# Hybrid decoder trunk, first stage: dt from raw x in fp32 on four column groups, and C's first tile beside B's

## The chip, the cores and the metric

The kernel runs on one core of a Trainium2 chip. The metric is device time in microseconds (us) of one execution of the whole program; a median over several runs is given. A profile is one further execution, recorded by the hardware profiler, with its own time. The engines are TensorE (PE, matrix products; PEld is its weight load), VectorE (DVE), ScalarE (ACT), GpSimd (POOL) and SyncE (SP), which here only starts transfers.

## The reference, cut to what matters

One layer of a decoder trunk: 528 tokens (16 learned meta tokens, then 512) of width 1024.

```python
u = rmsnorm(h, mix_norm_w[i])              # h * rsqrt(mean(h*h) + eps) * w
proj = u @ w_in[i]                         # 1024 x 9248
z = proj[..., OFF_Z:OFF_XBC]
xbc = proj[..., OFF_XBC:OFF_DT]            # x (2048), B (8 x 128), C (8 x 128)
dt_raw = proj[..., OFF_DT:OFF_GATE]        # 32 heads
gates = jax.nn.sigmoid(proj[..., OFF_GATE:] + b_gate[i])
...
xbc = jax.nn.silu(causal_depthwise_conv(xbc, conv_w, conv_b))
dt = jax.nn.softplus(dt_raw + dt_bias)
a_dt = dt * -jnp.exp(a_log)                # its cumulative sum per chunk of 128 is acs
y = ssd_chunked(xs, dt, a, b_mat, c_mat) + xs * d_skip[:, None]
...
h = h + (gate_pool * y_pool + gate_ssd * y_ssd) @ w_o[i]
v = rmsnorm(h, mlp_norm_w[i])
h = h + jax.nn.relu(v @ w_ff1[i]) ** 2 @ w_ff2[i]
out = rmsnorm(h, final_norm_w)[:, N_META:]
```

All is fp32.

## The kernel before, in words

**How products are made.** Activations lie transposed, channels on the partitions, in 8 tiles of 128 channels x 528 tokens. Most products are made from two halves: a value is cast to a shorter type (fp32r, "hi"), the rest is kept too ("lo"), and hi x hi, hi x lo and lo x hi are added in PSUM. So one product of 128 channels by 128 columns by a run of tokens is three matmuls. Weights come in blocks of 128 x 1024 (512 KB) in the order of use: `block_part` (L70) starts the transfer on SP's queue, ACT casts to `whi` (L73) and DVE subtracts to `wlo` (L74). Three raw blocks and four pairs of halves can be under way.

**The first stage.** Before the norm is known, projections run on x times the norm's weight (`xh`, `xl`, made from `xt` in `x_split`, L194 and L195) and are multiplied by the per-token scale `rsb` afterwards. Nine products of ones (L187) run while the first loads come. Then a loop over the 8 channel tiles k (L208 to L227): load `xt[k]`, split it, multiply it into `pdt` (dt) and `pB` (the first tile of B), and square it for the norm's sum `q` (on ACT and DVE). dt has only 32 columns of weights; they are repeated four times to fill 128 (`spread`, `once`, L184 to L208), so that all four chunks of 128 tokens find their dt on the partitions on which they are used. `dt_runs` are two runs of 272 and 256 tokens.

After the loop C's tile (`px0_24`), two tiles of x (`px0_0`, `px0_1`), z (`pz0`) and `GATES_FIRST` gates (`pgp`) follow on PE as group 0. Into them are woven, in the order in which a scheduler sees them ready: the sum of squares (`pn`, L244), the scale's broadcast (`pb`, L262, copied to `rsb` by ACT in L264), then DVE's chain for dt: `dv` (dt times the scale, L278 and L279), a softplus by a polynomial (L285 to L294, `ddt`), the cumulative sums (`dacs`, L299), and PE's transposes of both (`pt_dt`, L305). `norm_u` (L323 to L325) makes the normed `uh` and `ul` that all later projections read.

**After it.** For the groups g = 0 to 7 the state-space part of group g is woven with the projections of group g+1 (`px`, `pz`), and with one more gate where `GATE_AT` names one. L470 in there multiplies two heads of 64 channels into the two halves of one PSUM tile (`py`), in fp32. Pooling, the output product and the MLP follow.

**What sets the order.** Each engine works through its own list in order; the lists are made by a scheduler from the program's order and its own estimates, so a change in one place moves instructions around it. PSUM has two tiles of two banks (`psum2`: px, pz, pgp, pB) and four of one bank (`psum1`: pdt, pn, pb, pt_dt). SP starts transfers in order, POOL only a few.

Of the kernel before, what the change touches and what calls it, by code (L numbers as in the profile page):

```python
# [9 lines left out]
F32 = mybir.dt.float32  # L10
F32R = mybir.dt.float32r
AF = mybir.ActivationFunctionType
ALU = mybir.AluOpType

P = 128
D = 1024
SEQ = 512
NM = 16
# [18 lines left out]
V_N = 234  # L37


GATES_FIRST = 3  # L40
GATE_AT = {1: 3, 2: 4, 3: 5, 5: 6}
POOL_ORDER = (3, 2, 1, 0)
MERGE = (0, 4, 1, 5, 2, 6, 3, 7)

# [5 lines left out]
def kernel(ctx: ExitStack, tc, xT, x, w, vec, fnw, out):  # L50
# [12 lines left out]
    def block_tiles():  # L63
        b = nblk[0]
        nblk[0] += 1
        return (b, wp.tile([P, 1024], F32, tag="raw", name=f"raw{b}", bufs=3),
                wp.tile([P, 1024], F32R, tag="whi", name=f"whi{b}"),
                wp.tile([P, 1024], F32R, tag="wlo", name=f"wlo{b}"))

    def block_part(t, c):  # L70
        b, raw, hi, lo = t
        nc.sync.dma_start(raw[:, c], w[b, :, c])
        act.copy(hi[:, c], raw[:, c])  # L73
        dve.tensor_tensor(lo[:, c], raw[:, c], hi[:, c].bitcast(F32), op=ALU.subtract)  # L74

# [57 lines left out]
    def psum2(name):  # L133
        return psa.tile([P, 1024], F32, tag="mm", name=name)

    def psum1(name):
        return psb.tile([P, 512], F32, tag="s", name=name)
# [14 lines left out]
    def wide(ps, skip=0):  # L152

        h = (L - skip) // 2
        runs = [(ps[:, 512 - h : 512], slice(skip, skip + h)),
                (ps[:, 512 : 512 + h], slice(skip + h, L))]
        return runs, ps[:, 512 - h : 512 + h]
# [14 lines left out]
    H = HEADS  # L172


    pdt = [psum1(f"pdt{i}") for i in range(2)]
    dt_runs = [(pdt[0][:, : NM + 256], slice(0, NM + 256)), (pdt[1][:, :256], slice(NM + 256, L))]
    pB = psum2("px0_16")
    runsB, viewB = wide(pB)

    wdt, wB = block_tiles(), block_tiles()  # L180
    b, raw, hi, lo = wdt
    nc.sync.dma_start(raw[:, :256], w[b, :, :256])
    spread = lambda t: t.rearrange("p (k c h) -> p k c h", c=4, h=HEADS)
    once = raw[:, :256].rearrange("p (k h) -> p k h", h=HEADS).unsqueeze(2).to_broadcast([P, NK, 4, HEADS])  # L184

    for n in range(WARM):
        pe.matmul(pdt[1].rearrange("p (a b) -> p a b", a=4), ones_r,  # L187
# [2 lines left out]
    def x_load(k):  # L190
        nc.sync.dma_start(xt[k], xT[:, k, :])

    def x_split(k):
        act.activation(xh[k], xt[k], AF.Copy, scale=col(V_MIX, k))  # L194
        dve.scalar_tensor_tensor(xl[k], xt[k], col(V_MIX, k), xh[k].bitcast(F32),  # L195
                                 op0=ALU.mult, op1=ALU.subtract)

    x_load(0)
    act.copy(spread(hi)[:, :2], once[:, :2])
    dve.tensor_tensor(spread(lo)[:, :2], once[:, :2], spread(hi)[:, :2].bitcast(F32), op=ALU.subtract)  # L200
    x_split(0)
    block_part(wB, slice(0, 256))
    x_load(1)
    proj_step(dt_runs, 0, wdt[2:], X)
    proj_step(runsB, 0, wB[2:], X)
    x_split(1)
    act.copy(spread(hi)[:, 2:], once[:, 2:])
    dve.tensor_tensor(spread(lo)[:, 2:], once[:, 2:], spread(hi)[:, 2:].bitcast(F32), op=ALU.subtract)  # L208
    x_load(2)
    block_part(wB, slice(256, 1024))  # L210
    proj_step(dt_runs, 1, wdt[2:], X)
    proj_step(runsB, 1, wB[2:], X)
    def square(k):
        if k == 0:
            act.activation(q, xt[k], AF.Square)
# [5 lines left out]
    for k in range(2, NK):  # L221
        if k > 2:
            x_load(k)
        x_split(k)
        proj_step(dt_runs, k, wdt[2:], X)
        proj_step(runsB, k, wB[2:], X)
        square(k - 2)  # L227
    for k in (NK - 2, NK - 1):
        square(k)

# [43 lines left out]
    v, e, s, s2, pl, dt, acs = (dtile(n) for n in ("dv", "de", "ds", "ds2", "dpl", "ddt", "dacs"))  # L274
    for c in range(4):
        r = slice(c * H, (c + 1) * H)
        src = pdt[0][r, NM + c * P : NM + (c + 1) * P] if c < 2 else pdt[1][r, (c - 2) * P : (c - 1) * P]
        dve.tensor_tensor(v[r, :P], src, rsb[r, NM + c * P : NM + (c + 1) * P], op=ALU.mult)  # L278
    dve.tensor_tensor(v[:, P:], pdt[0][:, :NM], rsb[:, :NM], op=ALU.mult)  # L279
    act.activation(e, v, AF.Abs, bias=col(V_DTB, 0))  # L280
    act.activation(e, e, AF.Exp, scale=-1.0)
    ea = dp.tile([P, 1], F32, name="ea")
# [68 lines left out]
    def group_proj(g, cur, gate=None):  # L351

        first = g == 0
        xc, bt, ct, zt = cur
        for dst, t, skip in ((bt, 16 + g, 0), (ct, 24 + g, NM - 4), (xc[:, 0, :], 2 * g, 0),
                             (xc[:, 1, :], 2 * g + 1, 0)):
            if first and dst is bt:
                view = viewB
            else:
                runs, view = wide(psum2(f"px{g}_{t}"), skip)  # L360
                proj(runs, block(), X if first else U)
            conv(dst, first_raw(t, view, skip) if first else view, t)
            yield
        if gate is not None:
            gate_pool(gate)
            yield
        ps = psum2(f"pz{g}")
        for i in range(2):
            proj(narrow(ps[:, i * SEQ : (i + 1) * SEQ]), block(), X if first else U)
        zf = zt.rearrange("p i t -> p (i t)")  # L370
        if first:
            dve.tensor_tensor(zt, ps.rearrange("p (i t) -> p i t", i=2),
                              rsb[:, NM:].unsqueeze(1).to_broadcast([P, 2, SEQ]), op=ALU.mult)
            act.activation(zf, zf, AF.Silu)
        else:
            act.activation(zf, ps, AF.Silu)
        yield
# [829 lines left out]
```

## Time and profile before

| | us |
|---|---|
| median of 3 runs | 1025.1 (1024.82 to 1025.12) |
| the profiled execution | 1024.72 |
| its span, first to last instruction | 1023.0 |
| k loop of the first stage, first dt product to first C product | 5.5 to 18.3 |
| gates of the first stage, first product of `pgp` | 50.1 |
| first transposes of group 0 (L413) | 67.3 |
| PE, DVE, ACT busy | 1014.7, 739.4, 553.0 |

The granted clock of TensorE is 0.999 of full over the run. Views of the profile give times from the start of the span. A row of the timeline holds start, duration, engine, line, operation, output and inputs, sizes and count, and in brackets the idle time before it with what ended it. A q behind an engine is its instruction queue (SPq starts transfers). Matmuls overlap, so that the distance between starts, not the duration, is what one costs. A view by stretch gives, for each window, its length, then busy time and instructions of PE, PEld, DVE, ACT and POOL, the clock, and DMA. Waits are listed as total, count and longest.

### The profile page before, as it was taken

What the parts mean: (1) busy time and instruction counts of PE and PEld (TensorE: products, weight loads), DVE (VectorE), ACT (ScalarE), POOL (GpSimd) and SP (SyncE); (2) the same over time, 40 slices, a digit from 0 to 9 for tenths busy, and PEclk for the clock granted to TensorE, in tenths of its full rate; (3) what the DMA queues carried; (4) which work ended last, traced back from release to release, by engine and by line L of the source; (5) the groups of instructions that cost most, each with busy time, mean ns of one, the idle gap of its engine ahead of it and who ended that gap; (6) DMA issues with size and microseconds to landing.
All of it is one profiled execution on the core that took longest, in us unless ns stands there. A gap on an engine that the chain in (4) does not pass through costs nothing.

```text
span 1023.0 us, 14052 instructions
## 1 busy us (share of the span) xinstructions
PE 1014.7 (99%) x5697; PEld 878.0 (86%) x5697; DVE 739.4 (72%) x982; ACT 553.0 (54%) x728; POOL 9.9 (1%) x24
## 2 busy tenths in 40 slices
PE   9999999999999999999999999999999999999997
PEld 9889989998879898988899888888888888888886
DVE  7978788687746586978755457976686686776866
ACT  7775968586627339573244343475545355454444
POOL 0100000000000000000000001000000000000000
PEclk9999999999999999999999999999999999999999
DMA  6243051414332331414532333224323323334112
GB/s 238 72 159 104 21 165 41 146 46 140 103 102 85 103 104 42 145 42 140 189 102 85 103 104 119 87 90 157 103 83 106 121 82 112 96 102 124 42 42 83
DMA packets 29281, 105.62 MB, mean 103 GB/s; under 512 B 3297, under 2 KB 4257, under 8 KB 28193
## 3 DMA queue, kind: packets, MB, share of 16 engines
q1 hardware_dynamic: 26496, 92.75, 28.7%
q0 software_dynamic: 2000, 11.08, 2.9%
q8 instruction: 45, 0.74, 0.3%
q10 hardware_dynamic: 720, 0.91, 0.2%
q14 instruction: 20, 0.16, 0.0%
HBM read 102.55 MB, written 2.16 MB: 102 GB/s over the span
## 4 chain that ended last, share of the span: by engine, by line
PE 97%; DVE 2%; ACT 0%; issue 0%; ACTq 0%
PE px L143 6%; PE px L144 6%; PE pf L92 6%; PE px L146 6%; PE pf L91 6%; PE pf L90 6%; PE alpha L956 3%; PE alpha L957 3%; PE alpha L958 3%; PE pz L143 3%; PE pz L146 3%; PE pz L144 3%; PE py L470 2%; PE pso L90 2%; PE pp L144 2%; PE pp L146 2%
## 5 line engine op out<-in xcount | busy, mean ns | idle before, releaser
L73 ACT CAST whi<-raw 128x1024 fp32r<-128x1024 f32 (+1 forms) x131 | 135.7, 1043 | 231.5 <-PE pf L91 58.8
L74 DVE TENSOR_TENSOR wlo<-raw,whi 128x1024 fp32r<-128x1024 f32 (+1 forms) x131 | 158.4, 1212 | 125.1 <-ACT whi L73 117.8
L143 PE MATMUL px<-uh,whi 128*128 128x264 f32 (+1 forms) x448 | 121.2, 290 | 0.7 <-DVE ct L334 0.7
L144 PE MATMUL px<-ul,whi 128*128 128x264 f32 (+1 forms) x448 | 119.0, 286 | 0.0
L90 PE MATMUL pf<-vh,whi 128*128 128x512 f32 x256 | 99.8, 390 | 0.0
L92 PE MATMUL pf<-vh,wlo 128*128 128x512 f32 x256 | 99.7, 389 | 0.0
L91 PE MATMUL pf<-vl,whi 128*128 128x512 f32 x256 | 99.6, 389 | 0.0
L146 PE MATMUL px<-uh,wlo 128*128 128x264 f32 (+1 forms) x448 | 90.8, 284 | 0.0
L143 PEld LDWEIGHTS px<-uh,whi 128*128 128x128 f32 x448 | 84.6, 189 | 2.8 <-issue 2.6
L144 PEld LDWEIGHTS px<-ul,whi 128*128 128x128 f32 x448 | 84.9, 189 | 0.3
L146 PEld LDWEIGHTS px<-uh,wlo 128*128 128x128 f32 x448 | 69.4, 188 | 0.3 <-issue 0.3
L718 DVE TENSOR_TENSOR slo<-b,shi 128x1024 fp32r<-128x1024 f32 x35 | 42.6, 1217 | 31.7 <-ACT shi L717 31.7
L717 ACT CAST shi<-b 128x1024 fp32r<-128x1024 f32 x35 | 36.8, 1051 | 51.9 <-PE pf L91 36.5
L91 PEld LDWEIGHTS pf<-vl,whi 128*128 128x128 f32 x256 | 48.1, 188 | 10.0
L90 PEld LDWEIGHTS pf<-vh,whi 128*128 128x128 f32 x256 | 48.1, 188 | 9.9
L92 PEld LDWEIGHTS pf<-vh,wlo 128*128 128x128 f32 x256 | 48.1, 188 | 9.9
L956 PE MATMUL alpha<-shi,hh 128*128 128x512 f32 x140 | 54.6, 390 | 0.0
L957 PE MATMUL alpha<-slo,hh 128*128 128x512 f32 x140 | 54.5, 389 | 0.0
L958 PE MATMUL alpha<-shi,hl 128*128 128x512 f32 x140 | 54.5, 389 | 0.0
L783 DVE TENSOR_TENSOR ht<-ht,alpha 128x1024 f32<-128x1024 f32 x35 | 42.5, 1214 | 6.1 <-PE alpha L958 6.1
L143 PE MATMUL pz<-uh,whi 128*128 128x512 f32 x112 | 44.0, 393 | 0.0
L144 PE MATMUL pz<-ul,whi 128*128 128x512 f32 x112 | 43.9, 392 | 0.0
(412 smaller groups left out, 2451.4 us busy)
## 6 DMA issues: line engine op xcount, KB each, us to landing
raw<-in_w SPq DMA_DIRECT2D x129, 512.0 KB, 3.6
b<-in_w SPq DMA_DIRECT2D x28, 512.0 KB, 3.6
abc<-acs_d POOLq DMA_DIRECT2D x8, 1024.0 KB, 7.2
wob<-in_w SPq DMA_DIRECT2D x8, 512.0 KB, 4.6
xt<-in_xT SPq DMA_DIRECT2D x8, 264.0 KB, 5.3
ht<-in_x POOLq DMA_DIRECT2D x4, 512.0 KB, 6.0
w<-in_w SPq DMA_DIRECT2D x4, 512.0 KB, 3.5
out_dram<-out SPq DMA_DIRECT2D x4, 320.0 KB, 2.3
```

The lines of the kernel that those rows point to most:

```text
L73: act.copy(hi[:, c], raw[:, c])
L74: dve.tensor_tensor(lo[:, c], raw[:, c], hi[:, c].bitcast(F32), op=ALU.subtract)
L90: pe.matmul(ps, ah, bh, start=first, stop=False)
L91: pe.matmul(ps, ah, bl, start=False, stop=False)
L92: pe.matmul(ps, al, bh, start=False, stop=last)
L143: pe.matmul(o, wh, rhs[0][k][:, c], start=k == 0, stop=False)
L144: pe.matmul(o, wh, rhs[1][k][:, c], start=False, stop=False)
L146: pe.matmul(o, wl, rhs[0][k][:, c], start=False, stop=k == NK - 1)
L718: dve.tensor_tensor(lo, src, hi.bitcast(F32), op=ALU.subtract)
L956: pe.matmul(ps[t], a[0], wh[:, cs], start=f, stop=False, skip_group_check=True)
L957: pe.matmul(ps[t], a[0], wl[:, cs], start=False, stop=False, skip_group_check=True)
L958: pe.matmul(ps[t], a[1], wh[:, cs], start=False, stop=l, skip_group_check=True)
```

## The change

dt's weights are loaded unsplit and once (128 x 8 x 32, `wdt`), DVE multiplies them by the norm's weight, and dt is made from raw `xt` in plain fp32: in `dt_step`, after k = 3 and k = 7, the four channel tiles of a half of the loop write four different groups of 32 PSUM partitions, for two runs of 264 tokens (`HF`). Each group of partitions then holds the sum over two channel tiles. ACT copies the result to SBUF (`dtp`), and 8 small fp32 products with `e32` (four stacked 32 x 32 identities, made on DVE) add the four groups and put each chunk where it is used (`pdv`), from which `dv` is read.

In the k loop C's first tile takes dt's place beside B's (`bc_step`), with C's weights loaded and split in pieces of 256, 256 and 512 columns as B's now are, between the loads of x. dt's weights are asked for behind the second pieces. The tables of gates change, so that one more gate is computed in the first stage, from x, and none in the stage of group 5.

```diff
--- before.py
+++ after.py
@@ -37,8 +37,8 @@
 V_N = 234
 
 
-GATES_FIRST = 3
-GATE_AT = {1: 3, 2: 4, 3: 5, 5: 6}
+GATES_FIRST = 4
+GATE_AT = {1: 4, 2: 5, 3: 6}
 POOL_ORDER = (3, 2, 1, 0)
 MERGE = (0, 4, 1, 5, 2, 6, 3, 7)
 
@@ -67,9 +67,15 @@
                 wp.tile([P, 1024], F32R, tag="whi", name=f"whi{b}"),
                 wp.tile([P, 1024], F32R, tag="wlo", name=f"wlo{b}"))
 
+    def block_load(t, c):
+        nc.sync.dma_start(t[1][:, c], w[t[0], :, c])
+
     def block_part(t, c):
+        block_load(t, c)
+        block_split(t, c)
+
+    def block_split(t, c):
         b, raw, hi, lo = t
-        nc.sync.dma_start(raw[:, c], w[b, :, c])
         act.copy(hi[:, c], raw[:, c])
         dve.tensor_tensor(lo[:, c], raw[:, c], hi[:, c].bitcast(F32), op=ALU.subtract)
 
@@ -172,16 +178,19 @@
     H = HEADS
 
 
+
+    HF = (slice(0, HALF), slice(HALF, L))
     pdt = [psum1(f"pdt{i}") for i in range(2)]
-    dt_runs = [(pdt[0][:, : NM + 256], slice(0, NM + 256)), (pdt[1][:, :256], slice(NM + 256, L))]
-    pB = psum2("px0_16")
-    runsB, viewB = wide(pB)
-
-    wdt, wB = block_tiles(), block_tiles()
-    b, raw, hi, lo = wdt
-    nc.sync.dma_start(raw[:, :256], w[b, :, :256])
-    spread = lambda t: t.rearrange("p (k c h) -> p k c h", c=4, h=HEADS)
-    once = raw[:, :256].rearrange("p (k h) -> p k h", h=HEADS).unsqueeze(2).to_broadcast([P, NK, 4, HEADS])
+    pB, pC = psum2("px0_16"), psum2("px0_24")
+    (runsB, viewB), (runsC, viewC) = wide(pB), wide(pC, NM - 4)
+    b = nblk[0]
+    nblk[0] += 1
+    wdt = pre.tile([P, NK, H], F32, name="wdt")
+    wB, wC = block_tiles(), block_tiles()
+    e32 = pre.tile([P, H], F32, name="e32")
+    dve.tensor_tensor(e32, ident[:, :H], ident[:, H : 2 * H], op=ALU.add)
+    for c in (2, 3):
+        dve.tensor_tensor(e32, e32, ident[:, c * H : (c + 1) * H], op=ALU.add)
 
     for n in range(WARM):
         pe.matmul(pdt[1].rearrange("p (a b) -> p a b", a=4), ones_r,
@@ -195,21 +204,29 @@
         dve.scalar_tensor_tensor(xl[k], xt[k], col(V_MIX, k), xh[k].bitcast(F32),
                                  op0=ALU.mult, op1=ALU.subtract)
 
+    def dt_step(kb):
+
+        for i, run in enumerate(HF):
+            for c in range(4):
+                k = kb + c
+                pe.matmul(pdt[i][c * H : (c + 1) * H, :HALF], wdt[:, k, :], xt[k][:, run],
+                          start=kb == 0, stop=kb == 4, skip_group_check=True)
+
+    def bc_step(k):
+        proj_step(runsB, k, wB[2:], X)
+        proj_step(runsC, k, wC[2:], X)
+
     x_load(0)
-    act.copy(spread(hi)[:, :2], once[:, :2])
-    dve.tensor_tensor(spread(lo)[:, :2], once[:, :2], spread(hi)[:, :2].bitcast(F32), op=ALU.subtract)
     x_split(0)
-    block_part(wB, slice(0, 256))
+    for t in (wB, wC):
+        block_part(t, slice(0, 256))
     x_load(1)
-    proj_step(dt_runs, 0, wdt[2:], X)
-    proj_step(runsB, 0, wB[2:], X)
+    bc_step(0)
     x_split(1)
-    act.copy(spread(hi)[:, 2:], once[:, 2:])
-    dve.tensor_tensor(spread(lo)[:, 2:], once[:, 2:], spread(hi)[:, 2:].bitcast(F32), op=ALU.subtract)
     x_load(2)
-    block_part(wB, slice(256, 1024))
-    proj_step(dt_runs, 1, wdt[2:], X)
-    proj_step(runsB, 1, wB[2:], X)
+    for t in (wB, wC):
+        block_part(t, slice(256, 512))
+    bc_step(1)
     def square(k):
         if k == 0:
             act.activation(q, xt[k], AF.Square)
@@ -222,9 +239,23 @@
         if k > 2:
             x_load(k)
         x_split(k)
-        proj_step(dt_runs, k, wdt[2:], X)
-        proj_step(runsB, k, wB[2:], X)
+        if k == 2:
+            nc.sync.dma_start(wdt.rearrange("p k h -> p (k h)"), w[b, :, : NK * H])
+            dve.tensor_tensor(wdt, wdt, vs[:, V_MIX : V_MIX + NK].unsqueeze(2).to_broadcast([P, NK, H]), op=ALU.mult)
+        if k == 4:
+            for t in (wB, wC):
+                block_part(t, slice(512, 1024))
+        bc_step(k)
+        if k % 4 == 3:
+            dt_step(k - 3)
         square(k - 2)
+    dts_ = pre.tile([P, L], F32, name="dtp")
+    for i, run in enumerate(HF):
+        act.copy(dts_[:, run], pdt[i][:, :HALF])
+    pdv = psum1("pdv")
+    for o, n, at in ((0, P, lambda c: NM + c * P), (P, NM, lambda c: 0)):
+        for c in range(4):
+            pe.matmul(pdv[c * H : (c + 1) * H, o : o + n], e32, dts_[:, at(c) : at(c) + n], start=True, stop=True)
     for k in (NK - 2, NK - 1):
         square(k)
 
@@ -274,9 +305,8 @@
     v, e, s, s2, pl, dt, acs = (dtile(n) for n in ("dv", "de", "ds", "ds2", "dpl", "ddt", "dacs"))
     for c in range(4):
         r = slice(c * H, (c + 1) * H)
-        src = pdt[0][r, NM + c * P : NM + (c + 1) * P] if c < 2 else pdt[1][r, (c - 2) * P : (c - 1) * P]
-        dve.tensor_tensor(v[r, :P], src, rsb[r, NM + c * P : NM + (c + 1) * P], op=ALU.mult)
-    dve.tensor_tensor(v[:, P:], pdt[0][:, :NM], rsb[:, :NM], op=ALU.mult)
+        dve.tensor_tensor(v[r, :P], pdv[r, :P], rsb[r, NM + c * P : NM + (c + 1) * P], op=ALU.mult)
+    dve.tensor_tensor(v[:, P:], pdv[:, P : P + NM], rsb[:, :NM], op=ALU.mult)
     act.activation(e, v, AF.Abs, bias=col(V_DTB, 0))
     act.activation(e, e, AF.Exp, scale=-1.0)
     ea = dp.tile([P, 1], F32, name="ea")
@@ -354,8 +384,8 @@
         xc, bt, ct, zt = cur
         for dst, t, skip in ((bt, 16 + g, 0), (ct, 24 + g, NM - 4), (xc[:, 0, :], 2 * g, 0),
                              (xc[:, 1, :], 2 * g + 1, 0)):
-            if first and dst is bt:
-                view = viewB
+            if first and (dst is bt or dst is ct):
+                view = viewB if dst is bt else viewC
             else:
                 runs, view = wide(psum2(f"px{g}_{t}"), skip)
                 proj(runs, block(), X if first else U)
```

In the changed program the order on PE is: the k loop with the first dt step behind k = 3 and the second behind k = 7; `px0_0`, into which the 8 small products and `pn` are put after its first 8 matmuls and `pb` after 24 more; `px0_1`; `pz0`, with the transposes of `ddt` after 43 of its 48 matmuls; four gates. On ACT the order behind the last square is the copies of B's and C's PSUM tiles, one weight cast, the two copies of dt. On DVE the steps between `dv` and `ddt` are, beside the chain itself, four raw multiplications by `rsb`, eleven convolution steps, one product of `norm_u` and one weight split; before the change they were four, eight, three and one.

## The prediction

> **What bounds the kernel now.** I read the engine shares first, then the chain that ended last, then who TensorE (PE) waited for.
>
> ```profile
> span 1023.0 us, 14052 instructions
> PE 1014.7 (99%) x5697; PEld 878.0 (86%) x5697; DVE 739.4 (72%) x982; ACT 553.0 (54%) x728; POOL 9.9 (1%) x24
> ...
> PE 97%; DVE 2%; ACT 0%; issue 0%; ACTq 0%
> ```
>
> ```profile
> PE pdt L187 <- DVE ones_r L100: 1.5, 1, 1.5
> PE px L143 <- DVE ct L334: 0.7, 1, 0.7
> PE pt_dt L305 <- DVE ddt L294: 0.2, 1, 0.2
> ```
>
> PE holds 97% of the chain, and all its waits together are 2.4 us. So PE time that is taken away shows in the end one for one, and time that is added too, unless another engine is late. The second and third waits are the only places where DVE is late.
>
> The stage of the change, in the timeline (start, duration, engine, line):
>
> ```profile
> 16.83 0.29 PE L143 MATMUL pdt<-xh,whi 128*128 128x272 f32 x1
> ...
> 17.55 0.28 PE L143 MATMUL px<-xh,whi 128*128 128x264 f32 x1
> ...
> 18.27 0.28 PE L143 MATMUL px<-xh,whi 128*128 128x258 f32 x1
> ...
> 18.99 0.28 PE L143 MATMUL px<-xh,whi 128*128 128x258 f32 x1
> ...
> 20.54 1.09 PE L244 MATMUL pn<-ones_f,q 128*88 128x1 f32 x12
> 21.49 0.36 PE L144 MATMUL px<-xl,whi 128*128 128x258 f32 x1
> ...
> 25.54 0.28 PE L143 MATMUL px<-xh,whi 128*128 128x264 f32 x1
> ...
> 31.41 0.28 PE L143 MATMUL px<-xh,whi 128*128 128x264 f32 x1
> ```
>
> Durations overlap, so I go by starts. The last k step gives dt 0.72 us (16.83 to 17.55) and B 0.72 us (17.55 to 18.27); a step of C takes 0.72 us as well (18.27 to 18.99), and a whole px tile of 48 matmuls 5.87 us (25.54 to 31.41), 0.122 us each.
>
> **What it removes.** dt's 48 matmuls: 8 steps of 0.72 = 5.76 us of PE. C takes their place in the k loop, in k step 0 too, where everything runs at about half the pace; C's own 48 matmuls are only moved, so they cost nothing either way.
>
> **What it adds on PE.** 16 fp32 matmuls of 264 columns, each writing 32 partitions, and 8 small ones that add the four partial sums. The trace has no matmul of 32 columns of weights. The nearest is py (L470), fp32 with 64, whose two heads write different halves of PSUM. From the chain, in order of time:
>
> ```profile
> 74.15 0.89 PE pcb L442 x8
> 75.67 1.49 PE pst L451 x6
> ...
> 83.14 1.02 PE py L470 x16
> ...
> 131.36 0.80 PE py L470 x10
> 137.73 0.58 PE py L470 x6
> ```
>
> An fp32 matmul is two records: pcb's four matmuls are 8 records, 0.111 us each at 128 columns; pst's are 0.248 us at 256. That is 1.07 ns a column, so 0.257 us at 264; twice the 0.122 us of a px matmul gives 0.244. I take 0.25. py has 128 columns too, yet its 16 records take 0.064 us each: the two halves run at once. How they do shows in the counts: 8, 5 and 3 matmuls take 1.02, 0.80 and 0.58 us, equal steps of 0.22 us. The fuller half has 4, 3 and 2 matmuls in them, thus 8, 6 and 4 records: 0.11 us each, and the other half is free. So the time is that of the records in the fullest column group. What a visit costs beyond that:
>
> ```profile
> 82.76 0.38 PE L464 MATMUL po<-ct,st 128*128 128x128 f32 x2
> 83.07 1.09 PE L470 MATMUL py<-abc,xdt 128*64 128x128 f32 x16
> 84.09 0.94 PE L464 MATMUL po<-ct,st 128*128 128x128 f32 x6
> ```
>
> Two po records from 82.76 would end at 82.98; py starts 0.09 later. py then takes 1.02 to the next start, 0.14 over 8 records of 0.11. So a visit to narrow columns costs 0.23 us.
>
> A dt step has 8 matmuls, 2 to each of four groups, so 4 records deep: 4 x 0.25 + 0.23 = 1.23 us, two of them 2.46. The sums: 2 records of 128 columns (0.22) and 2 of 16 columns, priced by pn (12 records of one column in 20.54 to 21.49, 0.08 each, 0.16), and a visit: 0.61. Added 3.07 us; the bounds are full serial work (32 x 0.25 + 0.46 = 8.5, and 8 x 0.11 + 8 x 0.08 + 0.23 = 1.8) above and 2.7 us below, if the visits are half as dear. I take the four-wide value, because py shows groups that do not hold each other up.
>
> The Trainium skill prices this otherwise: in "TensorE: Matmul & The Clock Gate", Part 3, the table of measured speedups gives three column tiles 2.38 times, 0.79 of the ideal. No row here has more than two groups, and py's two reach 0.111 against 0.064, 1.73 times, or 0.87. By the page's 0.79 the two dt steps would be an estimated 3.0 us instead of 2.46 and the end 0.5 us later.
>
> PE balance: 3.07 - 5.76 = **-2.69 us**.
>
> **Feeding the k loop.** The 128 KB of dt weights ahead of x is joined by 512 KB of C, and SP issues 15 transfers instead of 11 ahead of the first px tile. What is behind them in SP's queue are x3 to x7.
>
> ```profile
> 3.60 2.64 SPq L191 DMA_DIRECT2D xt<-in_xT  x5
> ```
>
> ```profile
> DMA to landing us min/median/max: 3.1/5.3/5.8
> ```
>
> ```profile
> 14.13 0.72 ACT L194 ACTIVATE xh<-xt,vs 128x528 fp32r<-128x528 f32 x1
> ```
>
> ```profile
> 5.92 0.42 DVE L74 TENSOR_TENSOR wlo<-raw,whi 128x256 fp32r<-128x256 f32 x1
> ...
> 9.53 0.95 DVE L74 TENSOR_TENSOR wlo<-raw,whi 128x768 fp32r<-128x768 f32 x1
> ...
> 15.59 0.76 DVE L195 SCALAR_TENSOR_TENSOR xl<-xt,vs,xh 128x528 fp32r<-128x528 f32 x1
> ```
>
> An issue takes 0.53 us; the last x was issued by 6.2 us, and four more make it 8.4, landing at about 14 by the largest 5.8, where ACT took it at 14.13 before. DVE trades splits of 256+768 columns (1.37) for 256+256+512 of C (0.42 x 2 + 0.6) and cuts B into the same pieces; with the product of dt's weights (0.42) and three sums of 32 columns it has about 1.1 us more ahead of the last xl, which then ends at 17.4 instead of 16.35. PE wants it at 16.83 + 1.23 (the first dt step) + 0.12 = 18.2. Cover 0.8 us; without it, every late xl delays PE one for one. The tight one is xl3, which PE reaches at about 10.9, before any dt step, and which I get at 10.85. I take 0, bounds 0 and +1.
>
> **The added path of dt.** ACT must copy both halves out of PSUM before the sums, and PE reaches those 8 matmuls after the last dt step (0.97 us). Queued behind on PE are pn, all the px work and the norm.
>
> ```profile
> 26.21 0.65 ACT L264 COPY rsb<-pb 128x264 f32<-128x264 f32 x2
> ```
>
> ```profile
> 25.26 1.05 ACT L73 CAST whi<-raw 128x1024 fp32r<-128x1024 f32 x1 [2.39 <-PE px L144]
> ```
>
> Two such copies are 0.65 us and fit, but in ACT's order a weight cast of 1.05 us stands ahead of them. It starts once C has left PSUM (0.6 us), that is about when the dt step ends. I take 0.2 us of wait, bounds 0 and 0.5.
>
> **The norm chain and the extra gate.** pn now comes behind the whole k loop, dt and the sums, so the scale rsb and everything DVE does with it start no earlier, while PE is ahead.
>
> ```profile
> 26.34 1.23 DVE L74 TENSOR_TENSOR wlo<-raw,whi 128x1024 fp32r<-128x1024 f32 x1 [1.42 <-ACT whi L73]
> 27.49 1.18 DVE L278 TENSOR_TENSOR dv<-pdt,rsb 32x128 f32<-32x128 f32 x4
> ...
> 30.20 1.44 DVE L323 SCALAR_TENSOR_TENSOR xt<-xt,vs,rsb 128x528 f32<-128x528 f32 x2
> ...
> 42.44 0.75 DVE L334 SCALAR_TENSOR_TENSOR xc<-raw,vs,xc 128x526 f32<-128x526 f32 x1
> 43.12 0.29 DVE L294 SCALAR_TENSOR_TENSOR ddt<-dpl,dv 128x144 f32<-128x144 f32 x1
> ```
>
> ```profile
> 37.28 0.40 PE L143 MATMUL pz<-xh,whi 128*128 128x512 f32 x1
> ...
> 42.78 0.39 PE L143 MATMUL pz<-xh,whi 128*128 128x512 f32 x1
> ...
> 43.56 0.30 PE L305 MATMUL pt_dt<-ident,ddt 128*128 128x128 f32 x1 [0.16 <-DVE ddt L294]
> ```
>
> Before, ddt was ready 21.9 us after pn's end (43.41 against 21.49). The copies to rsb (26.21) stood behind the weight cast of 25.26, dv behind the split of 26.34. In the changed order neither does (1.2 us sooner), and DVE has three more convolution steps (xc, L334) and two fewer norm products (xt, L323) in between, 0.6 us more by the steps from start to start; so 21.3. PE's work between pn and that transpose is, in the changed order, 40 px matmuls, the norm's broadcast (0.7), a px tile and 43 pz matmuls of 0.229 (24 of them from 37.28 to 42.78): 4.9 + 0.7 + 5.87 + 9.85 = 21.3. So it still meets within some 0.2 us, as before: 0, bounds -0.3 and +1. The gate that is computed early costs the same 24 matmuls in either place; where it is taken out (the stage of group 5), PE must not run dry. Stages with and without one, in the table by stretch (PE busy first, DVE third, ACT fourth):
>
> ```profile
> 348.80:398.40 49.60, 49.60 (x347) 44.95 (x345) 35.73 (x55) 27.54 (x39) 0.53 (x1) 1.00 0.23 75
> 398.40:440.00 41.60, 41.60 (x310) 38.59 (x309) 32.40 (x51) 27.39 (x34) 0.53 (x1) 1.00 0.37 115
> ```
>
> Group 6 has no gate, and PE never stops in it; DVE stands at 32.4 of 41.6. Group 5 without its gate falls to some 44 us with DVE at 35.7: 0.
>
> **Sum.** -2.69 + 0.2 = -2.5 us. The profiled execution took 1024.72 us, span 1023.0 and 1.7 around it; that becomes 1022.2 (span 1020.5). The median of the runs shown, 1025.1, is 0.4 above the profiled execution, so I forecast **1022.6 us**.
>
> **Rivals.**
>
> *Two groups at a time.* What holds in py for two may be the limit for four. Then a dt step is 8 records deep (2.23 us) and the sums 0.99: 5.45 - 5.76 + 0.2 = -0.1, **1025.0 us**. For it: no row has more than two groups at once. Against it: py's groups are independent, and nothing in the rows shows a shared resource at its end. The Trainium skill has a rule that would bring the same: "TensorE: Matmul & The Clock Gate", Part 3, The mechanism, says that matmuls start and end strictly in program order. The second record of a matmul would then hold up the next group, and n matmuls of py would take n+1 records: 9, 6, 4. The trace has equal steps, 8, 6, 4, so it does not bear the rule out here.
>
> *Slower: dt's own chain is late.* Place: PE's transpose of ddt, with all of pz and the gates behind it. Price: one for one. Before, DVE ended 0.16 us too late, so there is no reserve. It decides from 2.5 us of lateness. If pn waits for the copies and sums, the three convolution steps (0.7 each) are not made up for by the earlier rsb, and two 1.2 us splits come between, ddt is 2.1 + 2.4 = 4.5 late: **1027.1 us**. Against it: the count above, which meets.
>
> *Part of the gain is lost* to late x splits (up to 1 us) and to the copies (0.3 over what I take): up to 1.3 us more, I say **1023.7**.
>
> *All groups in turn.* 8.5 + 1.8 - 5.76 = +4.5, and 0.2 of wait: **1029.8**. py's rows speak against it.
>
> *More gain.* The 0.7 us wait behind ct falls away as DVE's phase shifts, and the three visits cost half (0.35 less): **1021.5**.
>
> **How the numbers follow.** Forecast 0.62 (own range 1021.8 to 1023.4), two at a time 0.13, part lost 0.10, more gain 0.05, dt late 0.07, in turn 0.03. A measurement of this kernel can tell 0.2%, 2.05 us, from no change, so faster is below 1023.05. Of the forecast 0.56 lies there and 0.06 above; with the case of more gain that is 0.61 faster. Same: 0.06 + 0.13 + 0.10 = 0.29. Slower: 0.10. The range reaches down to the case of more gain and up past two at a time: 1021.0 to 1025.4, some 0.88 of the chance.
>
> **What would show it.** In the changed profile: the 16 dt records of a step start in fours, 0.25 us between fours, and a step takes 1.2 us from its first start to the next B matmul (2.2: two at a time; over 4: in turn). The first px tile starts at about 20.5 us, the second at 28.7 instead of 31.4. PE's waits name ACT's copy of dt with 0.2 us, and ddt with about 0.2. Group 5 has no wait. A wait of PE on xl or on x, or over 1 us on ddt, would make the forecast wrong; so would a new wait behind group 5's shorter stage.

## The result, and the profile after

| | before | after |
|---|---|---|
| median | 1024.87 us (1024.43 to 1025.67, 20 runs) | 1023.36 us (1022.92 to 1023.83, 20 runs) |
| profiled span | 1023.0 | 1021.8 |
| time outside the span, median | 1.72 | 1.96 |

The ratio is 0.9985 (95% interval 0.9978 to 0.9992): the change wins 1.5 us, where I forecast 2.5. It lies inside the range, but also inside what I had called no change (2.05 us); I had given "faster" 0.61 and "same" 0.29. An execution at a lowered clock, one in run 7 and one in run 11, is left out of the intervals and spreads below and moves no median by more than 0.07 us. From the page of the changed kernel, engine shares and chain:

```profile
span 1021.8 us, 14071 instructions
PE 1013.0 (99%) x5697; PEld 872.7 (85%) x5697; DVE 739.7 (72%) x988; ACT 550.6 (54%) x729; POOL 10.0 (1%) x24
...
PE 98%; DMA 1%; DVE 1%; ACT 0%; issue 0%; SPq 0%; ACTq 0%
```

PE still sets the end; DMA has 1% of the chain now, and DVE's 2% have become 1%. Whom PE waited for, beside the wait for `ones_r` ahead of the loop, which is as before (total, times, longest):

```profile
PE px L149 <- DVE ct L364: 0.7, 1, 0.7
PE px L150 <- DVE xl L204: 0.4, 1, 0.4
PE px L149 <- ACT xh L203: 0.2, 1, 0.2
PE py L500 <- issue: 0.2, 1, 0.2
```

The wait for ddt is gone, the one for ct is as before, and three are new. The timeline of PE in the first stage of the changed kernel:

```profile
10.91 0.39 PE L149 MATMUL px<-xh,whi 128*128 128x264 f32 x1 [0.22 <-ACT xh L203]
11.71 0.39 PE L150 MATMUL px<-xl,whi 128*128 128x264 f32 x1 [0.41 <-DVE xl L204]
...
13.24 1.10 PE L212 MATMUL pdt<-xt,wdt 128*32 128x264 f32 x16
14.27 0.39 PE L149 MATMUL px<-xh,whi 128*128 128x264 f32 x1
14.50 0.28 PE L150 MATMUL px<-xl,whi 128*128 128x264 f32 x1
...
22.46 0.52 PE L258 MATMUL pdv<-dtp,e 128*32 128x128 f32 x16
22.91 1.10 PE L275 MATMUL pn<-ones_f,q 128*88 128x1 f32 x12
```

The 16 records of a dt step are done in 1.03 us from the first start to the next matmul of B; with the 0.09 us that PE takes to enter, that is 1.12. It is not all: the matmul behind the step is 0.23 us ahead of the next one (14.27 to 14.50) instead of 0.12, and so it is behind the second step (21.29 to 21.51). With these 0.11 a step costs PE 1.23 us. The sums cost 0.45 and 0.09; behind them stands `pn`, whose 12 records take 0.97 us to the next matmul (0.95 before). There is no wait ahead of `pdv`. The wait of k step 3 stands at the top: xh and xl of x3 (the load of `xt[3]`) come late, and by starts PE loses 1.06 us there.

The transpose of ddt, rows of DVE and PE from the timeline:

```profile
44.54 0.32 DVE L324 SCALAR_TENSOR_TENSOR ddt<-dpl,dv 128x144 f32<-128x144 f32 x1
45.16 0.27 PE L335 MATMUL pt_dt<-ident,ddt 128*128 128x128 f32 x1
```

ddt ends 0.3 us ahead of PE, where it had ended 0.16 too late. So dt's chain meets, as counted.

Judged by the first transpose of B in group 0 (66.60 before, 70.14 after, with one gate of 5.50 us more), the first stage won 1.96 us in this execution. Its span of 1021.8 is one of the longest of the 20 (1021.1 to 1021.9, median 1021.4). In runs 1, 3 and 4 below, which run the same instructions up to 46 us, the first stage won 2.47, 2.49 and 2.01. The rest was lost late. The stages of groups 5, 6 and 7, each from its first transpose of B (the last to the first `psl`), by stretch: length, busy time and instructions of PE, PEld, DVE, ACT, POOL. Before:

```profile
347.99:397.63 49.64, 49.64 (x345) 44.99 (x344) 35.23 (x55) 27.58 (x39) 0.53 (x1) 1.00 0.23 75
397.63:441.18 43.55, 43.55 (x321) 40.19 (x320) 32.95 (x52) 29.33 (x35) 0.53 (x1) 1.00 0.35 110
441.18:495.11 53.93, 53.93 (x321) 46.61 (x320) 44.88 (x61) 24.63 (x34) 0.00 (x0) 1.00 0.39 132
```

After:

```profile
351.55:395.69 44.14, 44.14 (x322) 40.48 (x321) 30.09 (x48) 22.15 (x29) 0.53 (x1) 1.00 0.26 84
395.69:439.96 44.27, 44.27 (x322) 40.45 (x320) 36.40 (x55) 30.46 (x39) 0.53 (x1) 1.00 0.30 96
439.96:494.12 54.16, 53.96 (x321) 46.63 (x320) 45.09 (x63) 25.75 (x37) 0.00 (x0) 1.00 0.39 132
```

Group 5 falls by exactly its gate, 5.50 us. But 5.1 us of DVE's work went out of it (35.23 to 30.09) and 3.5 us came into group 6, which now takes 0.72 us more for the same matmuls, and group 7 takes 0.23 more. What PE does there shows in the timeline of group 6, before:

```profile
414.33 1.09 PE L470 MATMUL py<-abc,xdt 128*64 128x128 f32 x16
415.35 0.39 PE L143 MATMUL px<-uh,whi 128*128 128x264 f32 x1
```

and after, with one row of group 7 below:

```profile
412.37 0.37 PE L149 MATMUL px<-uh,whi 128*128 128x264 f32 x1
412.67 0.65 PE L500 MATMUL py<-abc,xdt 128*64 128x128 f32 x6
413.25 0.49 PE L494 MATMUL po<-ct,st 128*128 128x128 f32 x2
413.67 0.87 PE L500 MATMUL py<-abc,xdt 128*64 128x128 f32 x10
414.46 0.39 PE L150 MATMUL px<-ul,whi 128*128 128x264 f32 x1
...
453.37 1.09 PE L500 MATMUL py<-abc,xdt 128*64 128x128 f32 x16 [0.20 <-issue]
```

The scheduler laid py's 16 records in two visits, with a matmul of px ahead and two of po between them. Sums over the group by tile, start to start: py 0.36 us more, px 0.27, po 0.11. PE was busy all the time, so no wait shows it. In group 7 PE stops ahead of py, 0.20 us in the row above and 0.27 by starts; "issue" says that the profile names nothing that it waited for.

### The profile page after: what moved, and what is told of

Read it like the earlier page. It is cut to its first block, busy times and chain, and to the rows that moved or that the text cites. A ratio compares the mean times of both kernels' runs of the same rounds, so it can differ in the third digit from the quotient of the medians.

```text
span 1021.8 us, 14071 instructions
## 1 busy us (share of the span) xinstructions
PE 1013.0 (99%) x5697; PEld 872.7 (85%) x5697; DVE 739.7 (72%) x988; ACT 550.6 (54%) x729; POOL 10.0 (1%) x24
## 4 chain that ended last, share of the span: by engine, by line
PE 98%; DMA 1%; DVE 1%; ACT 0%; issue 0%; SPq 0%; ACTq 0%
PE px L149 6%; PE px L150 6%; PE px L152 6%; PE pf L98 6%; PE pf L96 6%; PE pf L97 6%; PE alpha L986 3%; PE alpha L988 3%; PE alpha L987 3%; PE pz L149 3%; PE pz L150 3%; PE pz L152 3%; PE py L500 2%; PE pso L96 2%; PE pp L150 2%; PE pp L152 2%
```

## The experiments

"Before" is the kernel of before on the same chip in the same session (1024.65 to 1024.93 us).

| what | median us | ratio to before, 95% |
|---|---|---|
| 1 changed, gate tables of before | 1022.33 | 0.9976 (0.9967 to 0.9986) |
| 2 before, changed gate tables | 1025.97 | 1.0010 (1.0001 to 1.0019) |
| 3 changed, no gate in group 1 instead of 5 | 1022.04 | 0.9974 (0.9963 to 0.9984) |
| 4 changed, no gate in group 2 instead of 5 | 1023.97 | 0.9991 (0.9982 to 0.9999) |
| 5 changed, dt's weights behind x3 | 1023.26 | 0.9985 (0.9976 to 0.9994) |
| 6 changed, x3 between B's and C's second pieces | 1023.49 | 0.9987 (0.9978 to 0.9995) |
| 7 as 3 and 5 together | 1022.23 | 0.9974 (0.9963 to 0.9984) |
| 8 changed, dt step issued group by group | 1023.34 | 0.9986 (0.9977 to 0.9995) |
| 9 dt on four column groups alone | 1024.64 | 1.0002 (0.9993 to 1.0011) |
| 10 C beside B alone | 1027.40 | 1.0027 (1.0016 to 1.0037) |
| 11 as 10, ACT's copies sooner | 1025.71 | 1.0008 (0.9999 to 1.0017) |
| 12 the kernel of 11 once more | 1025.84 | 1.0009 (0.9999 to 1.0018) |

Each interval is 1.7 to 2.2 us wide; differences below 1 us between two of these kernels rest on their medians (8 to 11 runs, each spread over 0.5 to 1.3 us, 11 and 12 over 2.2 and 2.4) and on the trace.

### The gate of group 5 (runs 1 and 2)

```diff
-GATES_FIRST = 4
-GATE_AT = {1: 4, 2: 5, 3: 6}
+GATES_FIRST = 3
+GATE_AT = {1: 3, 2: 4, 3: 5, 5: 6}
```

> The changed kernel with the gate tables of before (three gates first, one in group 5); all the rest as changed. Theory: about 1 us was lost where group 5 has no gate, because the scheduler puts work between matmuls there. Then the stretch from the first transpose of group 5 (ptb) to the first matmul behind the groups (psl) takes 147.1 us as before, group 0's ptb starts at 64.6 us (66.6 before, less the 2.0 won in the first stage), and the kernel takes 1 us less than the changed one: 1022.4. Rival 1: the loss has another cause (DVE's phase against PE, set by the earlier start); then the stretch takes 148.1 us and the time stays at 1023.4. Rival 2: the first stage needs the fourth gate as cover for the norm and the first u; then ptb or the first px of group 1 waits up to 1 us, the stretch is 147.1 us and the time is 1023.4 too.

1022.33 us. The three stages of groups 5 to 7 together, from the view by stretch of run 1:

```profile
sum 147.13, PE 147.13 PEld 131.78 DVE 113.03 ACT 81.55 POOL 1.06; mean PE 49.04 PEld 43.93 DVE 37.68 ACT 27.18 POOL 0.35
```

147.13 us, 147.12 before. Group 0's first transpose starts at 64.13, and neither it nor the first px of group 1 waits. So the theory holds, and the fourth gate was not needed as cover. The time falls by 1.03 us. The span falls by more (medians 1020.0 and 1021.4), and the time outside it grows by 0.34 (2.30 and 1.96), which stays unexplained. Run 2 is the same edit on the kernel of before, the other way round:

> The kernel of before with the changed gate tables alone (four gates first, none in group 5). Theory: taking the gate out of group 5 costs 0.95 us by itself: the stretch from ptb of group 5 to psl takes 142.6 us instead of the 141.6 that 147.1 less the gate's 5.5 would give, and the time is 1025.8 against 1024.9 of before. Rival: a gate costs the same in either place; 141.6 us and 1024.9.

1025.97, 1.2 us above before. The stretch took 142.57 us, 4.55 less for a gate that costs 5.50. So 0.95 us belong to the gate tables and not to dt or C; the other 0.2 are lost in the first stage, which is 5.71 us longer for a gate of 5.50.

### Is it group 5, or any group? (runs 3 and 4)

```diff
-GATE_AT = {1: 4, 2: 5, 3: 6}
+GATE_AT = {2: 4, 3: 5, 5: 6}
```

> The changed kernel with four gates first, but the group without a gate is group 1 instead of group 5 (gates in groups 2, 3 and 5). Theory: the 0.95 us belong to taking a gate out of any group: group 1 to the end of the groups (ptb of group 1 to psl) takes 380.4 us, 5.5 less than with all gates (385.0 with the gates of before) and 0.95 more; the time is 1023.4. Rival: they belong to group 5 and the groups behind it, where the scheduler moved the norm of group 5 into group 6: then 379.5 us and 1022.4.

1022.04 us: the rival. From the transposes of group 1 to psl it takes 379.5 us, 5.5 less than with all gates. The stages of groups 1 and 2, by stretch:

```profile
113.17:158.19 45.02, 44.34 (x322) 40.49 (x321) 37.37 (x59) 33.55 (x46) 0.53 (x1) 1.00 0.31 94
158.19:207.53 49.34, 49.34 (x346) 44.77 (x345) 40.52 (x60) 35.99 (x49) 0.53 (x1) 1.00 0.28 86
```

Here too DVE's work goes out of the group (42.44 us before) and into the next (36.42 before, 4.1 more). But PE loses nothing by it: group 2 takes 0.29 us less than before (49.63), since one py of it is whole that was in two visits before, and group 3 takes 0.42 more, since one of its is torn instead. Run 4 takes the gate from group 2 instead (`{1: 4, 3: 5, 5: 6}`):

> The changed kernel with four gates first and no gate in group 2 (gates in groups 1, 3 and 5). Theory: the loss is tied to group 5 and what follows it, where no later group has a gate and the order of py was split; with the gate back in group 5 it is gone whichever other group is without one: ptb of group 5 to psl takes 147.1 us, the time is 1022.0 as with group 1. Rival: taking a gate out of a group costs something in most places, and group 1 was a lucky one: 1023.0 or more, with the loss between ptb of group 2 and ptb of group 5.

1023.97: here the rival again, and with it falls the idea that only group 5 is special. From ptb of group 5 to psl it takes 147.1 us, as expected, but the stage of group 3, behind the one without a gate, took 50.52 us, 1.43 more than before (49.09). By stretch, groups 2 and 3 of run 4, then the new wait in its timeline:

```profile
164.16:208.29 44.13, 44.13 (x322) 40.46 (x320) 32.55 (x51) 28.08 (x33) 0.53 (x1) 1.00 0.33 108
208.29:258.81 50.52, 49.84 (x345) 45.00 (x344) 42.44 (x65) 39.12 (x56) 0.53 (x1) 1.00 0.25 84
```

```profile
228.33 0.36 PE L149 MATMUL px<-uh,whi 128*128 128x264 f32 x1 [0.68 <-DVE ct L364]
```

The pattern is that of group 5: the group itself gets shorter by the gate's 5.50 us, DVE and ACT get less done in it (DVE 36.42 to 32.55), and the next group has it on top (39.35 to 42.44): py in one visit more (0.36 us) and a wait for ct. Group 1 gave its gate away for less than 0.1 us. So in all three places DVE's work moves one group on; what PE loses by it was 0.95, 1.43 and under 0.1 us, and with it goes whether py came out torn. Why the scheduler lays py whole in one place and torn in another, these runs do not show.

### x3's late landing (runs 5, 6 and 7)

SP's issues and what ACT and DVE waited for in the changed kernel, from the timeline:

```profile
4.37 0.33 SPq L243 DMA_DIRECT2D wdt<-in_w  x1
4.74 0.91 SPq L200 DMA_DIRECT2D xt<-in_xT  x2
...
10.12 1.41 ACT L203 ACTIVATE xh<-xt,vs 128x528 fp32r<-128x528 f32 x2 [0.93 <-DMA xt<-in_xT]
10.89 0.77 DVE L204 SCALAR_TENSOR_TENSOR xl<-xt,vs,xh 128x528 fp32r<-128x528 f32 x1 [0.87 <-ACT xh L203]
```

x3 is issued at 4.74 us (3.60 before) and lands at 10.09 (8.80 before). Run 5 moves dt's weights behind it, run 6 moves x3 further ahead:

```diff
-        if k == 2:
+        if k == 3:
             nc.sync.dma_start(wdt.rearrange("p k h -> p (k h)"), w[b, :, : NK * H])
...
```

> The changed kernel with the load of dt's weights and the product with them one k step later, behind the load of x3. x3 then is issued at about 4.4 us instead of 4.74 and has 128 KB fewer ahead of it. Theory: PE's wait of 1.06 us in k step 3 is x3's landing, set by what stands ahead of it in SP's queue; x3 lands 0.4 to 0.7 us sooner, the wait shrinks to 0.4 to 0.7 and the time to 1022.8. Rival 1: the bytes of B's and C's second pieces ahead set the landing, and one small transfer does not matter: wait and time as in the changed kernel, 1023.4. Rival 2: the wait goes but comes back, as dt's weights are late for the first dt step at 13.1 us or the norm chain meets at the transpose of ddt: 1023.4 with a new wait named there.

```diff
-    for t in (wB, wC):
-        block_part(t, slice(256, 512))
+    block_part(wB, slice(256, 512))
+    x_load(3)
+    block_part(wC, slice(256, 512))
...
-        if k > 2:
+        if k > 3:
             x_load(k)
```

> The changed kernel with the load of x3 between the second pieces of B and C, two places sooner in SP's queue: issued at about 3.6 us instead of 4.74. Theory: it lands at about 7.5 us, where C's second piece landed, PE does not wait in k step 3, and the time falls by up to 1.06 us: 1022.3. Rival 1: C's second piece, now behind x3, is late for k step 2 instead, and the wait only moves: 1023.4. Rival 2: the time won ahead is lost at the transpose of ddt, whose chain starts with the last x: 1023.4, with a wait on ddt of over 0.5 us.

1023.26 and 1023.49 us against 1023.36: nothing. x3 did land sooner (9.19 and 8.44 us), and the stop in k step 3, which all five profiled executions with x3 in its place have, is gone. But PE waits in k step 1, in the timeline of run 5:

```profile
7.83 0.39 PE L150 MATMUL px<-xl,whi 128*128 128x264 f32 x1 [0.26 <-DVE xl L204]
```

In run 5 the span did fall by 0.4 us (median 1021.0 against 1021.4), but the time outside it grew by 0.27 (2.23 against 1.96). Run 7 was to separate this on the better gate tables:

> The changed kernel with two edits together: no gate in group 1 instead of group 5 (1022.0 us alone), and dt's weights loaded behind x3 (1023.3 alone, against 1023.4 of the changed kernel). Theory: x3's landing still costs part of the first stage in every execution; with it sooner the span falls by 0.4 us, as it did alone: 1021.6. Rival: the waits for x in the k loop only move from one k step to another, since all of x and the weights come through at one rate: 1022.0, no gain over the gate alone.

1022.23, not below the 1022.04 of run 3: the rival. Its own wait is in k step 1 too, and so is that of run 3, which leaves x3 where it was. First run 7, then run 3:

```profile
8.27 0.39 PE L150 MATMUL px<-xl,whi 128*128 128x264 f32 x1 [0.41 <-DVE xl L204]
```

```profile
8.00 0.39 PE L150 MATMUL px<-xl,whi 128*128 128x264 f32 x1 [0.42 <-DVE xl L204]
```

A measure without regard to the place: before, k step 4 starts at 12.41 us; with one dt step more ahead of it, 13.53 would be level. With x3 in its place the changed kernel stands at 14.27 there, runs 1, 3, 4 and 8 at 13.85, 13.76, 14.23 and 14.01; with x3 sooner runs 5, 6 and 7 stand at 13.35, 13.82 and 13.74. So the loop loses some 0.3 us, from -0.2 to 0.7 by execution. One execution each can't tell whether x3's place is worth some tenths of that; in the times it does not show.

### Do the column groups run freely? (run 8)

```diff
-        for i, run in enumerate(HF):
-            for c in range(4):
+        for c in range(4):
+            for i, run in enumerate(HF):
```

> The changed kernel; within a dt step the 8 matmuls are issued column group by column group (both halves of a group one behind the other) instead of all four groups in turn. Theory 1: each column group works off its own records, whatever stands between in the program: a dt step takes 1.1 us from its first start to the next matmul of B, as in the changed kernel, and the time is 1023.4. Theory 2: records start in the order of the program, so that a group that is busy holds up the next: 13 records deep instead of 4, a step takes 1.1 + 9 x 0.22 = 3.1 us, the time is 1027.3. Between: two groups overlap, some 2 us a step, 1025.

1023.34 us, and a step, in the timeline of run 8:

```profile
12.95 1.12 PE L212 MATMUL pdt<-xt,wdt 128*32 128x264 f32 x16
14.01 0.39 PE L149 MATMUL px<-xh,whi 128*128 128x264 f32 x1
```

1.06 us instead of 1.03. The records still start in fours, 13 ns apart within a four (7 ns with the groups in turn), and 0.22 to 0.25 us from one four to the next. In the program a group's four records stand one behind the other, so a record of the next group must have started ahead of them. Theory 1 holds.

### One part without the other (runs 9 to 12)

Run 9 leaves C's first tile behind the loop (`bc_step` without `runsC`) and has the gate tables of before.

> The changed kernel with the other part alone: dt in fp32 on four column groups, its sums by PE; the first tile of C behind the loop as before, the gate tables of before. A k step of PE is then 0.7 us of B; the scheduler lays dt's matmuls and the sums between B's. Theory: ACT needs 1.4 us for each x (split 0.73, square 0.63) and DVE as much, so PE waits in the loop for about what dt's matmuls had taken, C begins at about 18.3 us as before, and the time stays within 0.5 us of 1024.8. Rival: the work taken away comes off the end at any rate, and 2.5 us are won as with both parts: 1022.3.

1024.64 us, level with before. PE's timeline in its k loop:

```profile
9.01 0.39 PE L150 MATMUL px<-xl,whi 128*128 128x264 f32 x1 [0.41 <-DVE xl L204]
...
9.94 1.08 PE L212 MATMUL pdt<-xt,wdt 128*32 128x264 f32 x10
...
11.76 0.65 PE L212 MATMUL pdt<-xt,wdt 128*32 128x264 f32 x6
```

The first step is torn into 10 and 6 records, which cost 1.10 and 0.67 us (9.73 to 10.95 and 11.55 to 12.34 from the start ahead to the start behind, less a matmul of 0.12 each), 1.8 instead of 1.12; the second is torn into 2, 8 and 6. From 9.73 to 15.73 us PE does these 32 records and 14 matmuls of B, of 0.121 us each: the five visits cost 4.3 us, two whole ones 2.5. So most of what dt saved goes into torn visits, and no long wait shows. Whole steps would not have brought all of it back, for the last x comes late, in DVE's timeline:

```profile
15.58 0.76 DVE L204 SCALAR_TENSOR_TENSOR xl<-xt,vs,xh 128x528 fp32r<-128x528 f32 x1
```

It ends at 16.34 us. Five matmuls of B (0.6) have to follow it, and with the sums (0.6) behind them as here C could begin at 17.5 at the soonest; it began at 18.27, as before. So of the 2.8 us that dt needs less, some 2 would have gone into waiting for x with only 0.72 us of B per k step, an estimate from these rows and not shown by a run. The first transpose of group 0 starts at 66.60 us, to the hundredth as before.

Run 10 is the other half on the kernel of before:

```diff
+    for t in (wB, wC):
+        block_part(t, slice(0, 256))
...
     proj_step(runsB, 0, wB[2:], X)
+    proj_step(runsC, 0, wC[2:], X)
```

> The kernel of before with one part of the change alone: the first tile of C beside B's, with the weights in the same pieces; dt in halves as before (48 matmuls in the k loop), the gate tables of before. Theory: C's matmuls are only moved, and k steps of 2.2 us leave x time to land, so PE does not wait and nothing is won: 1024.8, as before. Rival 1: the norm chain, which now starts behind a loop that is 5.9 us longer, is late for the transpose of ddt: a wait on ddt there and 1026 or more. Rival 2: a part of the gain of the change comes from C's place itself: below 1024.0.

1027.40, 2.75 us slower, and by none of the three. The wait in PE's timeline, then ACT's:

```profile
26.34 0.39 PE L143 MATMUL px<-xh,whi 128*128 128x264 f32 x1 [1.58 <-ACT raw L355]
```

```profile
22.23 1.99 ACT L73 CAST whi<-raw 128x1024 fp32r<-128x1024 f32 x2 [3.17 <-PE pdt L144]
24.24 1.28 ACT L256 ACT_TABLE_LOAD   x1
25.54 0.26 ACT L256 ACTIVATE rs<-pn,eps 88x6 f32<-88x6 f32 x1
25.70 1.07 ACT L355 COPY raw<-px 128x528 f32<-128x528 f32 x2
```

The two-bank PSUM tiles are two, and B and C hold both. The first px tile needs B's copied out, and ACT has two casts, a table load and the square root ahead of that copy. After this stop PE does not come back at full pace, by stretch (the number behind POOL's is the granted clock):

```profile
24.50:26.30 1.80, 0.25 (x4) 0.16 (x3) 1.57 (x5) 1.79 (x4) 0.00 (x0) 1.00 0.37 68
26.30:27.50 1.20, 1.17 (x9) 1.17 (x10) 1.20 (x3) 1.20 (x2) 0.00 (x0) 1.00 0.89 345
27.50:30.70 3.20, 3.20 (x17) 3.20 (x17) 3.05 (x8) 1.28 (x4) 0.00 (x0) 0.51 0.73 197
```

A clock of 0.51 for 3.2 us, and 15 matmuls of 0.22 instead of 0.12 us. Wait (from `pn` to the next start 2.62 us instead of 0.95, so 1.67) and pace (1.55) are 3.2 us; group 0 is 2.6 late, so some 0.6 was won elsewhere in the stage. In the changed kernel the two copies (L377) ran from 19.66 us, ahead of the table load at 22.48: the full change escapes this wait by ACT's order. Run 11 puts the copies ahead of the square root in the program:

```diff
+    raw0 = {}
+    for t, v, skip in ((16, viewB, 0), (24, viewC, NM - 4)):
+        raw0[t] = pre.tile([P, L - skip], F32, tag="raw0", name=f"raw0_{t}", bufs=4)
+        act.copy(raw0[t], v)
     for k in (NK - 2, NK - 1):
         square(k)
...
```

> The kernel of before with the first tile of C beside B's alone, as in the run that took 1027.4 us, but with ACT's two copies of B and C out of PSUM issued ahead of the square root of the norm. Theory: the 2.75 us lost there were PE's wait of 1.7 us for these copies, and the half pace of the 16 or so matmuls behind that stop (1.5 us more); ACT still has two weight casts ahead of the copies, so a wait of some 0.3 us is left, too short for the half pace: 1024.6, within 0.4 us of before. Rival 1: the pace stays low behind the short wait too: 1025.9. Rival 2: C's place costs by itself (the norm chain, the data): 1026 or more with another wait named.

1025.71 us, 1.7 less than run 10, 0.8 above before. Run 12 is the same kernel, and its profile is the one read here:

> The same kernel as the last but one (C beside B alone, ACT's copies of B and C ahead of the square root), which took 1025.7 us and left no profile at full clock. What is open is where the 0.9 us over before come from. Theory (rival 1 of that run): a short wait, up to 0.4 us, of PE for ACT's copies behind pn, and after it matmuls of px 0.1 us slower each for 16 to 20 matmuls; 1.9 us together, less 1.0 won ahead of it. Rival: no wait and full pace there, and the loss lies at the transpose of ddt or in the group stages: ptb of group 0 at 66.6 us as before, or a wait on ddt of about 0.9 us.

Neither, quite. PE behind `pn` in the timeline, and its wait in group 0:

```profile
23.89 1.03 PE L256 MATMUL pn<-ones_f,q 128*88 128x1 f32 x12
24.94 0.39 PE L143 MATMUL px<-xh,whi 128*128 128x264 f32 x1
```

```profile
PE po L478 <- DVE st L470: 0.4, 1, 0.4
```

The long stop and the low clock are gone, so they were what run 10 had lost up to group 0: it starts at 66.45 us, 2.75 sooner than in run 10 and 0.15 sooner than before. Then group 0 loses 0.4 for a state that DVE has late. This execution took 1025.27; the ten runs spread from 1024.83 to 1027.24, and what the longer ones have is not in this profile. That stays open.

## Why the prediction was right, and where it was not

**What dt costs: right.** I had 1.23 us for a dt step and 0.61 for the sums. Measured as I had measured py, from the end ahead to the first start behind, a step took 1.12; with the 0.11 that PE loses behind it, which that measure leaves out (behind py in group 6 before too: 415.35 to 415.58), it took 1.23. The records were a little faster than I had them, the visit a little dearer. The sums took 0.54. The balance is 2 x 1.23 + 0.54 - 5.76 = -2.76 instead of -2.69. The four groups run at once, and run 8 shows that not even the program's order matters within a step. So "two at a time" and "all in turn" are out. By the single price of 0.257 us from pst's rows, 16 records in 1.03 us are 4.0 times as fast as one by one, and 3.3 times with what the visit costs around them. The Trainium skill's 2.38 for three column tiles ("TensorE: Matmul & The Clock Gate", Part 3, the table of measured speedups) would have given an estimated 3.0 us for both steps; by the same measure they took 2.24. And its sentence that matmuls are in program order in start and end (Part 3, The mechanism) does not hold here for starts across column groups.

**The added path: right in kind.** The copies fit: ACT ended them at 22.46 us, just as PE got to `pdv`, and the wait of 0.2 us did not come, with nothing in hand. ddt met, 0.3 us in hand. The slower rival is out. Beside it stood a danger that I did not name: ACT's copies of B and C out of PSUM. 1.7 us late in run 10, they cost 3.2.

**Feeding the k loop: 0 was too low.** I had xl3 at 10.85 us with PE at 10.9. It was ready at 11.66 in the profiled execution, and the loop stands 0.7 us behind there, some 0.3 in the middle of the eight profiled executions of this loop (the changed kernel and runs 1 to 8 without run 2). x3's landing is what the trace names; loading it sooner takes that stop away and is worth nothing that the times show. With -2.76 and these 0.3 the first stage should win some 2.45 us; it wins 2.0 to 2.7, 2.4 in the middle. That is nearly the forecast's number, and in part by luck: the 0.2 us of wait that did not come and the sums stand against the 0.3 that did.

**The step that failed: "Group 5 without its gate falls to some 44 us with DVE at 35.7: 0."** It fell to 44.14. But I looked at the stage that loses the gate, and the bill came in the next two: 0.72 and 0.23 us. Without the gate's 5.50 us of PE work, 3.5 us of DVE's work come one group later; py is torn, and its narrow visit is paid twice. Runs 1, 2 and 4 show the loss from three sides. These 0.95 us are the missing 1.0: with the gates of before the change takes 1022.33, a gain of 2.46 where I had forecast 2.5. That agreement is closer than the evidence: by span run 1 gains some 3 us, and 0.6 go to time outside the span. That DVE's later work is what makes the scheduler tear py is argued and not shown, and run 3 speaks against a simple rule: as much work moves there, and nothing is lost.

Two of the signs that I had named as making the forecast wrong did come: PE waits for x (0.4 and 0.2 us), and there is a new stop behind group 5's shorter stage. The measured time stands nearer to the rival "part of the gain is lost" (1023.7) than to the forecast. Its late splits are part of the loss; the larger part, in groups 6 and 7, was in none of the rivals.

**Why the whole was more than its parts.** Neither part wins alone (1024.64 and 1025.7 against 1024.65 to 1024.93). By the rows of run 9, dt's saving is only time if other PE work fills the loop while x lands and is split, which C does, and if dt's steps stay whole, which they do beside C; C's move by itself only shifts matmuls, and needs its copies out of PSUM in time. I had costed that move at nothing, which holds in this pair, but I did not say that the saving hangs on it.

**Not explained.** The time outside the span is 1.72 us before (1.66 to 1.75 in 31 runs), 1.96 after, 2.30 in run 1 and 1.75 in run 3. I took 1.7 for both. No view of the trace shows what it holds.

The best version is run 3, the change with the gate left out of group 1 instead of group 5: 1022.04 us, 1.3 below the changed kernel and 2.6 below before. Against run 1 it is better by 0.3 only through the time outside the span; run 1's span is the shorter one (medians 1020.0 and 1020.3).

## What to carry to other kernels

Where PE is the bound, taking its filler out of a stage can cost nothing in that stage and something in the next, where the work of the other engines moves and the order on PE changes; compare PE's order and DVE's busy time one stage on, and try each place. Work taken out of a loop that data feeds is only won if other PE work moves in, and a narrow product should stay in one piece. A wait that a fed loop shows at one k step differs in size and place by execution; read several before reordering loads for it.

## What the runs showed of the hardware that was not expected

- Four column groups of 32, in fp32, ran wholly at once: the records of a four start 7 ns apart, 0.22 to 0.25 us from one four to the next (changed kernel), and records of a later matmul overtake those of an earlier one that writes another group (run 8). Around such a stretch PE loses 0.09 us ahead and 0.11 behind.
- A stop of PE of 1.6 us, behind the one-column matmuls of `pn`, was followed by a granted clock of 0.51 for 3.2 us, beginning 1.2 us after PE was back (run 10); where PE went on 0.1 us late it stayed at full (run 12). One profiled execution each shows this. The Trainium skill ("TensorE: Matmul & The Clock Gate", Part 1) speaks of an idle window of about 3.4 us for that; here about half of it went ahead of the low clock.
- The first k step begins at half pace, 0.22 us a matmul, in all of these kernels, and the full pace comes by execution at 6.2 us (runs 3, 5, 7 and 8) to 7.7 (before).
